# Two of four column groups of a gate product move from TensorE to VectorE, and the down projection's partial sums stay ungated until the last third

## The chip, the cores and the metric

The kernel runs on one core of a Trainium2 chip. The metric is the time in microseconds (us) of one execution on the device, as the median of several runs. The engines are named as in the profile: PE is TensorE's matrix multiplication, PEld its weight load, DVE VectorE, ACT ScalarE, POOL GpSimd, and SP SyncE, whose queue issues nearly all loads from HBM.

## What is computed

One inference step of a trunk layer on 128 context tokens and 128 latent tokens, D = 2048, feed-forward width 5632, all in fp32. Cut to what this change touches:

```python
mod = SiLU(cond) @ w_mod + b_mod     # 2 conditions (context, latent), 6 x 2048 columns
shift1, scale1, gate1, shift2, scale2, gate2 = split(mod, 6)
...                                  # mixer: scan branch, attention branch, x += gate1 * (...)
xm2 = RMSNorm(x) * (1 + scale2) + shift2
x = x + gate2 * ConvFFN(xm2)         # up projection (2 x 5632), centred conv of width 3,
                                     # a * SiLU(b), down projection (5632 -> 2048)
y = RMSNorm(x)
```

The change lies in gate2: how its 2048 columns are computed, and where in the feed-forward part they are multiplied in.

## The kernel before

**Weights.** Every weight comes as a stream of 512 KB tiles `raw` (128 partitions, two k-tiles of 512 columns) through a ring of five buffers (`RAW`). SP's queue issues the loads in the order of the program's list of steps; a load waits until the tile whose buffer it takes over has been read. `drive()` splits each weight tile into a rounded part `hi` (ACT, a copy, L184) and a remainder `lo` (DVE, a subtraction, L185), three buffers of each (`HL`), and PE multiplies three times: hi by low part, lo by high part, hi by high part, as an fp32 product.

**Feed-forward part.** It runs in three thirds (`CUT`: 8, 7 and 7 groups of 256 hidden columns and their 256 partners). In each third all *up groups* come first (`up_group`, 8 weight tiles each, called units here; PE lines L395 to L397, 24 matmuls of 256 columns per unit), then four *down groups* (`down_group`, one for each 512 output columns; L421 to L423). An up group accumulates in two PSUM banks, `h=0` and `h=1`, of a pool `acc` of three; so the second bank of the next group is one that the group before still has to give back. `evac()` empties them at every group's edge: for each of four pieces ACT writes a scaled copy into `ab` (L903) and DVE adds the two neighbours of the convolution (L904, L905), then come a SiLU (L906), the product (L907), and the split of the result (L909, L910). PE works through the first units of a group with `h=0` of three units ahead of `h=1` of the same three.

**Modulation product.** `mod_steps` computes mod in column groups of 512: the weights are PE's moving operand, the two condition vectors sit in a stationary operand of 32 columns, and each k-tile is put on one of four 32-column strips of PE (L263, `mod_mm`; unsplit fp32). A block of two raw tiles makes eight records in the profile. `mod_pp` then transposes the sums on DVE (L268), adds the four strips on PE (L272) and the bias on DVE (L276). Groups 20 to 23 are gate2; their 16 blocks are woven between the up units of the first third. At the end of these ups `load_g2` transposes the gate into rows, writes them to DRAM, and loads them back as four broadcast tiles `g2` (`gate_rows`, `gate_load`).

**Down groups.** After each down group of each third `down_evac` multiplies the sums in PSUM by the gate (L925) and adds the result to the residual `x1t` (L926): two DVE operations of 128x512 for each of the two sequences. In the last third ACT also takes the sum of squares there (L928), for the final norm, and DVE multiplies by that norm's weights (L929).

**Order.** Each engine executes its instructions in the order in which the built program has them. That order is set when the program is built, by a scheduler with priorities: `hi` and `lo` get a raised one (`HP`), everything else goes by the order of the steps.

Of the kernel before, what the change touches and what calls it, by code (L numbers as in the profile page):

```python
# [10 lines left out]
F32 = mybir.dt.float32  # L11
F32R = mybir.dt.float32r
I32 = mybir.dt.int32
AF = mybir.ActivationFunctionType
# [76 lines left out]
ATTP, ATTH, OLS = 1, 300, False  # L91
FF0, FF1, MF0, MF1 = 0.0, 1.0, 0.0, 1.0
G2A, G2B, G2S, G2C, LAG2, HP2 = 8, 8, 3, 2, 2, 1000
FIRST_BANKS = ("acc", "acc", "acc", "y")


@with_exitstack
def tile_hybrid_step(ctx, tc, a):
# [17 lines left out]
    def T4(shape, name, dt=F32):  # L116
        return w4.tile(shape, dt, tag="w4", name=name)
# [18 lines left out]
    def step(fn):  # L136
        steps.append(Step(fn))
# [180 lines left out]
    def mod_first(k0, n):  # L318
        v = a["w_mod_first"]
        st = {}  # L320
        nk = 8 // n
        view = lambda raw: raw.rearrange("p a c -> p (a c)").rearrange("p (k c) -> p k c", k=nk)

        def chunk(part, ku):
            def f(raw):
                if part == 0 and ku == 0:
                    st["a"] = PS([128, 2, 128 * n], "mod")
                r = view(raw)
                for j in range(nk):
# [7 lines left out]
        return [Step(chunk(p, ku), src(p, ku), False, "w4") for p in range(2) for ku in range(2 * n)]  # L337

    small = cpool.tile([128, 16], F32, name="small")
    nT = []  # L340
# [577 lines left out]
    G2 = []  # L918
    gfb = []

    def down_evac(acc, cg, s, last):
# [5 lines left out]
        if last:  # L927
            ACT(t, xv, AF.Square, accum_out=fs[:, 4 * s + cg:4 * s + cg + 1])  # L928
            TT(xv, xv, gfb[cg // 2][:, cs], OP.mult)  # L929

    def down_group(cg, ka, kb, last):
        st = {}

        def chunk(k0):
            def f(hi, lo):
                if k0 == ka:
                    st["a"] = [PS([128, 512], "acc", 3) for _ in range(2)]
                as_unit(st["a"], hi, lo, ff_lhs, k0, ka, kb)
                if k0 + 2 == kb:
                    for s in range(2):  # L940
                        down_evac(st["a"][s], cg, s, last)
                    if last and cg == 2:
                        norm_pre()
                        ACT(warm, fs[:, 6:7], AF.Sqrt)
            return f
        return [Step(chunk(k0), wsrc(a["w_down"], k0, 512 * cg)) for k0 in range(ka, kb, 2)]

    def down_last(cg, ka, kb):
        st = {"w": []}

        def chunk(k0):
            def f(hi, lo):
                if k0 == ka:
                    st["a"] = [PS([128, 512], "acc", 3) for _ in range(2)]
                st["w"].append((hi, lo))
                as_unit(st["a"], hi, lo, ff_lhs, k0, ka, kb, (0,))
                if k0 + 2 == kb:
                    for s in range(2):
                        if s:
                            for i, w in enumerate(st["w"]):  # L960
                                as_unit(st["a"], *w, ff_lhs, ka + 2 * i, ka, kb, (1,))
                        with tc.high_priority(HP2):
                            down_evac(st["a"][s], cg, s, True)
                            final(s)
            return f
        u = [Step(chunk(k0), wsrc(a["w_down"], k0, 512 * cg)) for k0 in range(ka, kb, 2)]
        for x in u[:len(u) - HL]:
            x.hl = XM
        return u
# [6 lines left out]
            gfb.append(t)  # L976

    CUT = [0, 8, 15, 22]
    g2s = mod_steps([20, 21, 22, 23])
    for x in g2s[:G2B]:  # L980
        x.pool = "first"

    def load_g2():
        gate_rows(80)
        for cg in range(4):
            G2.append(T4([128, 2, 512], "g2"))
            gate_load(80, cg, G2[cg])

    def behind(u):
        f = u.fn  # L990
# [11 lines left out]
    for p in range(3):  # L1002
# [3 lines left out]
        if p == 0:  # L1006
# [21 lines left out]
        if p == 2:  # L1028
            step(load_gf)
        for cg in range(4):  # L1030
            steps.extend((down_last if (p, cg) == (2, 3) else lambda *x: down_group(*x, p == 2))(cg, 2 * CUT[p], 2 * CUT[p + 1]))

    yout = [a["y_prompt"].rearrange("o t c -> (o t) c"), a["y_sample"].rearrange("o t c -> (o t) c")]

# [469 lines left out]
```

## Time and profile before

| | |
|---|---|
| median of 3 runs | 1549.94 us (1549.81 to 1554.12) |
| the profiled execution | 1552.15 us, its span 1550.1 us, mean PE clock 0.99 |
| PE, PEld busy | 1491.0 us (96%), 1311.1 us (85%) |
| DVE, ACT busy | 1007.7 us (65%), 766.7 us (49%) |
| POOL busy | 85.7 us (6%) |
| feed-forward part, first third | ups about 776 to 977 us, downs to 1066 |
| second third | ups about 1068 to 1229 us, downs to 1306 |
| last third | 1306 to the end |

A group of rows names a line, an engine and an operation, its output and inputs, how often it ran, and the mean duration. In an engine's timeline a row has its start, its duration and, in brackets, the idle time of that engine before it and what ended it. Where instructions of one engine follow each other without a gap, the distance of their starts is shorter than the duration that is printed; that distance is called the pitch here.

### The profile page before, as it was taken

Reading aid. Unit: us, or ns where it says so; the run is one execution under the profiler, and the core shown is the slowest. Engines: PE = TensorE matmul, PEld = TensorE weight load, DVE = VectorE, ACT = ScalarE, POOL = GpSimd, SP = SyncE. Lnnn points to the kernel's source line nnn. Section 1 sums busy time; section 2 is a strip of 40 time slices with the busy share of each in tenths; the row PEclk is TensorE's granted clock in tenths of the full one; section 3 lists DMA queues with packets and bytes.
Section 4 is the critical chain, followed back from the end, with each engine's and each line's share of the span. In section 5 each row is a group of like instructions: output and inputs, shape, how many; then the busy total and the mean of one; then the engine's idle time right before and its main releaser. Section 6 shows DMA issues by size and latency. Waiting matters only on the chain.

```text
span 1550.1 us, 29294 instructions
## 1 busy us (share of the span) xinstructions
PE 1491.0 (96%) x11871; PEld 1311.1 (85%) x11871; DVE 1007.7 (65%) x1541; ACT 766.7 (49%) x1191; POOL 85.7 (6%) x179
## 2 busy tenths in 40 slices
PE   6989999999899999999999999999999999999997
PEld 5758799778677788998689999889999988999986
DVE  4997776468866566765665656655665655666665
ACT  6335537645545666544554544433544543545543
POOL 2000004022321000000000000000000000000000
PEclk9999999999999999999999999999999999999999
DMA  9999754774676677975566676765555565566563
GB/s 352 352 340 321 286 196 157 258 277 156 209 241 238 240 250 274 310 244 192 172 242 235 205 245 201 238 200 190 176 192 181 181 197 191 175 205 197 170 203 123
DMA packets 104246, 349.18 MB, mean 225 GB/s; under 512 B 13900, under 2 KB 16628, under 8 KB 104112
## 3 DMA queue, kind: packets, MB, share of 16 engines
q1 hardware_dynamic: 98576, 344.20, 64.9%
q0 software_dynamic: 5312, 3.05, 0.8%
q8 instruction: 93, 1.52, 0.4%
q14 instruction: 41, 0.34, 0.1%
q10 hardware_dynamic: 224, 0.08, 0.0%
HBM read 343.76 MB, written 2.46 MB: 223 GB/s over the span
## 4 chain that ended last, share of the span: by engine, by line
PE 83%; DMA 8%; DVE 4%; ACT 2%; issue 1%; POOL 1%; SPq 0%; DVEq 0%; ACTq 0%
PE acc L395 16%; PE acc L396 16%; PE acc L397 16%; PE acc L421 8%; PE acc L422 8%; PE acc L423 8%; PE mod L263 5%; DMA raw<-in_w_mod_dram 2%; DMA raw<-in_w_in_dram 2%; PE bu L1375 1%; DVE lo L185 1%; DMA rw<-in_w_mod_dram 1%; DMA U<-u 1%; DMA raw<-in_w_attn_o_dram 1%; ACT hi L184 1%
## 5 line engine op out<-in xcount | busy, mean ns | idle before, releaser
L185 DVE TENSOR_TENSOR lo<-raw,hi 128x1024 fp32r<-128x1024 f32 (+1 forms) x456 | 538.7, 1186 | 444.8 <-ACT hi L184 442.8
L184 ACT ACTIVATE hi<-raw 128x1024 fp32r<-128x1024 f32 (+1 forms) x456 | 468.5, 1029 | 609.1 <-PE acc L397 260.7
L395 PE MATMUL acc<-yh,lo 128*128 128x256 f32 x1408 | 400.0, 284 | 0.0
L396 PE MATMUL acc<-yl,hi 128*128 128x256 f32 x1408 | 398.8, 283 | 0.0
L397 PE MATMUL acc<-yh,hi 128*128 128x256 f32 x1408 | 398.7, 283 | 0.0
L395 PEld LDWEIGHTS acc<-yh,lo 128*128 128x128 f32 x1408 | 270.3, 192 | 8.9 <-DVE lo L185 4.2
L396 PEld LDWEIGHTS acc<-yl,hi 128*128 128x128 f32 x1408 | 270.3, 192 | 0.1
L397 PEld LDWEIGHTS acc<-yh,hi 128*128 128x128 f32 x1408 | 270.2, 192 | 0.0
L395 PE MATMUL acc<-xh,lo 128*128 128x256 f32 x568 | 166.8, 294 | 9.3 <-ACT sig L672 4.8
L396 PE MATMUL acc<-xl,hi 128*128 128x256 f32 x568 | 163.4, 288 | 0.0
L397 PE MATMUL acc<-xh,hi 128*128 128x256 f32 x568 | 163.1, 287 | 0.0
L422 PE MATMUL acc<-lo,ff 128*128 128x512 f32 x352 | 136.8, 389 | 0.0
L423 PE MATMUL acc<-hi,ff 128*128 128x512 f32 x352 | 136.8, 389 | 0.0
L395 PEld LDWEIGHTS acc<-xh,lo 128*128 128x128 f32 x568 | 109.2, 192 | 31.4 <-DVE lo L185 6.9
L421 PE MATMUL acc<-hi,ff 128*128 128x512 f32 x352 | 127.8, 390 | 0.0
L396 PEld LDWEIGHTS acc<-xl,hi 128*128 128x128 f32 x568 | 109.6, 193 | 2.4 <-issue 2.2
L397 PEld LDWEIGHTS acc<-xh,hi 128*128 128x128 f32 x568 | 109.5, 193 | 0.7 <-issue 0.7
L263 PE MATMUL mod<-raw,cst 128*32 128x512 f32 x480 | 72.2, 631 | 8.0 <-DMA raw<-in_w_mod_dram 7.2
L421 PEld LDWEIGHTS acc<-hi,ff 128*128 128x128 f32 x352 | 66.1, 188 | 14.7 <-issue 1.1
L423 PEld LDWEIGHTS acc<-hi,ff 128*128 128x128 f32 x352 | 66.1, 188 | 13.7
L422 PEld LDWEIGHTS acc<-lo,ff 128*128 128x128 f32 x352 | 66.1, 188 | 13.5
L1316 POOL DMA_DIRECT2D U<-u x128 | 62.6, 497 | 159.6 <-PE bu L1375 138.5
(365 smaller groups left out, 2149.3 us busy)
## 6 DMA issues: line engine op xcount, KB each, us to landing
raw<-in_w_up_dram SPq DMA_DIRECT2D x176, 512.0 KB, 4.2
raw<-in_w_mod_dram SPq DMA_DIRECT2D x120, 512.0 KB, 5.1
raw<-in_w_in_dram SPq DMA_DIRECT2D x88, 512.0 KB, 4.5
raw<-in_w_down_dram SPq DMA_DIRECT2D x88, 512.0 KB, 4.3
rw<-in_w_mod_dram SPq DMA_DIRECT2D x56, 512.0 KB, 6.6
raw<-in_w_out_dram SPq DMA_DIRECT2D x32, 512.0 KB, 4.1
rw<-in_w_mod_first_dram SPq DMA_DIRECT2D x16, 512.0 KB, 7.4
raw<-in_w_in_dram SPq DMA_DIRECT2D x32, 256.0 KB, 6.1
```

Source lines behind the costliest of these rows:

```text
L184: ACT(th[:, w], raws[n][:, w], AF.Copy)
L185: TT(tl[:, w], raws[n][:, w], f32(th[:, w]), OP.subtract)
L263: return MM(acc[32 * j:32 * j + 32], cst[:, kt, 6 - 2 * b:38 - 2 * b], rhs, start=start, stop=stop, skip_group_check=True, tile_position=( ...
L395: MM(o, wl, xh, start=start, stop=False, skip_group_check=True)
L396: MM(o, wh, xl, start=False, stop=False, skip_group_check=True)
L397: MM(o, wh, xh, start=False, stop=stop, skip_group_check=True)
L421: MM(accs[s], xl, hi[:, j, :], start=(kt == first), stop=False)
L422: MM(accs[s], xh, lo[:, j, :], start=False, stop=False)
L423: lastmm[0] = MM(accs[s], xh, hi[:, j, :], start=False, stop=(kt == last - 1))
L1316: nc.gpsimd.dma_start(G["U4", qd][32 * e:32 * e + 32, q, :], u[32 * q:32 * q + 32, 64 * e:64 * e + 64])
L1375: MM(bu[:, ri, x], BL[d][:, ri, q, :], u[:, :, ::-1] if d else u, start=(x == 0), stop=True, skip_group_check=True)
```

## The change

Three things are changed.

- **Product.** Groups 22 and 23 of the modulation product (`G2P`) leave PE. `vec_mod` loads the same 16 raw tiles through the same ring, now woven into the first 0.8 of the *second* third's up units, and DVE computes them as running sums: for each of the two groups a tile `pacc` with two rows of 512 columns per partition (one per condition), to which each of the 16 k-tiles is added as weights times a per-partition scalar. That is 4 `tensor_scalar` and 60 `scalar_tensor_tensor` (STT) of 128x512. `done()` then sums over the partitions with four PE matmuls against a one-column selector (`onesel`), and a second `mod_pp` follows.
- **Gate rows.** Writing the gate's rows moves from the end of the first third's ups to the end of the second third's ups; the broadcast loads to the start of the last third.
- **Down sums.** The first third's down sums are copied ungated from PSUM into four tiles `ysum` by ACT, the second third's are added to them by DVE (one operation instead of two), and at the start of the last third `gate_sum` multiplies by the gate and adds to `x1t`: 16 DVE operations of 128x512. The last third is as before.

```diff
+G2P, POOLMOD = (22, 23), False
+    def vec_mod(gs):
+        n = 8 * len(gs)
+        st = {"raw": {}, "acc": []}
+        src = lambda i: wsrc(a["w_mod"], 2 * (i % 8), 512 * MOD_AT[gs[i // 8]])
...
+        def product(i, r):
+            if i % 8 == 0:
+                st["acc"].append(S4([128, 2, 512], "pacc"))
+            acc = st["acc"][-1]
+            for j in range(2):
+                kt = 2 * (i % 8) + j
+                for x in range(2):
+                    c = cst[:, kt, 6 + x:7 + x]
+                    if kt == 0:
+                        MODENG.tensor_scalar(acc[:, x], r[:, j], c, None, op0=OP.mult)
...
+                    else:
+                        STT(acc[:, x], r[:, j], c, acc[:, x], op0=OP.mult, op1=OP.add)
...
+            return Step(lambda raw: product(i, raw), src(i), False)
+        def done():
+            p = PS([128, 512], "mod")
+            m = 2 * len(gs)
+            with tc.issue_after(lastmm[0].ins):
+                for r in range(m):
+                    j = r % 4
+                    MM(p[32 * j:32 * j + 32], onesel[:, 7 - r:39 - r], st["acc"][r // 2][:, r % 2, :], start=r < 4, stop=r + 4 >= m,
+                       skip_group_check=True, tile_position=(0, 32 * j))
+            mod_pp(p, len(gs), [(4 * gs[0], 0, 4, 0, len(gs))])
+        return [unit(i) for i in range(n)], done
...
+    def down_part(acc, cg, s, p):
+        if len(ysum) < 4:
+            ysum.extend(T4([128, 1024], "ysum") for _ in range(4))
+        y = ysum[2 * s + cg // 2][:, 512 * (cg % 2):512 * (cg % 2) + 512]
+        if p:
+            TT(y, acc, y, OP.add)
+        else:
+            ACT(y, acc, AF.Copy)
+    def gate_sum(cg):
+        cs = slice(512 * (cg % 2), 512 * (cg % 2) + 512)
+        for s in range(2):
+            y, xv = ysum[2 * s + cg // 2][:, cs], x1t[2 * s + cg // 2][:, cs]
+            TT(y, y, G2[cg][:, s, :], OP.mult)
+            TT(xv, xv, y, OP.add)
...
-    g2s = mod_steps([20, 21, 22, 23])
+    g2s = mod_steps([g for g in range(20, 24) if g not in G2P])
+    g2u, g2done = vec_mod(list(G2P))
...
             weave(ups[8 - LAG2:], (g2s, 0.0, 0.8))
-            step(load_g2)
+        elif p == 1:
+            weave(ups, (g2u, 0.0, 0.8))
+            step(g2done)
+            step(lambda: gate_rows(80))
         else:
+            for cg in range(4):
+                step(lambda cg=cg: load_g2(cg))
             steps.extend(ups)
```

Three places of the built program show how the instructions stand. Lines have moved in the changed kernel: L371 is an accumulation of the product on DVE, L959 and L960 are the former L904 and L905, L962 and L965 the former L907 and L910, L186 the former L185, and L450 to L452 the former L395 to L397.

The first place is VectorE at an edge between two up groups of the second third. Before:

```order
L904 SCALAR_TENSOR_TENSOR ab_12450<-acc_12214,cw_118,ab_12450 128x2x127
L905 SCALAR_TENSOR_TENSOR ab_12450<-acc_12214,cw_118,ab_12450 128x2x127
L185 TENSOR_TENSOR lo_12469<-raw_12304,hi_12468 128x1024
L904 SCALAR_TENSOR_TENSOR ab_12450<-acc_12215,cw_118,ab_12450 128x2x127
L904 SCALAR_TENSOR_TENSOR ab_12450<-acc_12214,cw_118,ab_12450 128x2x127
L905 SCALAR_TENSOR_TENSOR ab_12450<-acc_12215,cw_118,ab_12450 128x2x127
L905 SCALAR_TENSOR_TENSOR ab_12450<-acc_12214,cw_118,ab_12450 128x2x127
L904 SCALAR_TENSOR_TENSOR ab_12450<-acc_12215,cw_118,ab_12450 128x2x127
L905 SCALAR_TENSOR_TENSOR ab_12450<-acc_12215,cw_118,ab_12450 128x2x127
L907 TENSOR_TENSOR ab_12450<-ab_12450 128x512
L185 TENSOR_TENSOR lo_12501<-raw_12334,hi_12500 128x1024
```

The third edge of the second third in the changed kernel:

```order
L959 SCALAR_TENSOR_TENSOR ab_12414<-acc_12153,cw_121,ab_12414 128x2x127
L960 SCALAR_TENSOR_TENSOR ab_12414<-acc_12153,cw_121,ab_12414 128x2x127
L186 TENSOR_TENSOR lo_12459<-raw_12345,hi_12458 128x1024
L959 SCALAR_TENSOR_TENSOR ab_12414<-acc_12154,cw_121,ab_12414 128x2x127
L371 SCALAR_TENSOR_TENSOR pacc_12377<-raw_12388,cst_105,pacc_12377 128x512 x2
L959 SCALAR_TENSOR_TENSOR ab_12414<-acc_12153,cw_121,ab_12414 128x2x127
L960 SCALAR_TENSOR_TENSOR ab_12414<-acc_12154,cw_121,ab_12414 128x2x127
L371 SCALAR_TENSOR_TENSOR pacc_12377<-raw_12388,cst_105,pacc_12377 128x512 x2
L960 SCALAR_TENSOR_TENSOR ab_12414<-acc_12153,cw_121,ab_12414 128x2x127
L959 SCALAR_TENSOR_TENSOR ab_12414<-acc_12154,cw_121,ab_12414 128x2x127
L960 SCALAR_TENSOR_TENSOR ab_12414<-acc_12154,cw_121,ab_12414 128x2x127
L962 TENSOR_TENSOR ab_12414<-ab_12414 128x512
```

Four accumulations now stand inside the evacuation of the banks.

The second place is SP's queue in the same stretch, where every row loads a weight tile. Before:

```order
L155 DMA raw_11874<-in_w_up_dram 128x1024
L155 DMA raw_11904<-in_w_up_dram 128x1024
L155 DMA raw_11952<-in_w_up_dram 128x1024
L155 DMA raw_11984<-in_w_up_dram 128x1024
L155 DMA raw_12014<-in_w_up_dram 128x1024
```

In the changed kernel:

```order
L156 DMA raw_12345<-in_w_up_dram 128x1024
L156 DMA raw_12375<-in_w_up_dram 128x1024
L156 DMA raw_12386<-in_w_up_dram 128x1024
L156 DMA raw_12388<-in_w_mod_dram 128x1024
L156 DMA raw_12462<-in_w_up_dram 128x1024
L156 DMA raw_12492<-in_w_up_dram 128x1024
L156 DMA raw_12502<-in_w_mod_dram 128x1024
L156 DMA raw_12504<-in_w_up_dram 128x1024
L156 DMA raw_12558<-in_w_up_dram 128x1024
```

The modulation tiles stand between the up weights. A load waits for the buffer that it takes over: that of raw_12502 for raw_12388's, which the last accumulation in the rows above frees. VectorE's next rows there are these:

```order
L371 SCALAR_TENSOR_TENSOR pacc_12377<-raw_12502,cst_105,pacc_12377 128x512 x2
L186 TENSOR_TENSOR lo_12489<-raw_12375,hi_12488 128x1024
L371 SCALAR_TENSOR_TENSOR pacc_12377<-raw_12502,cst_105,pacc_12377 128x512
L965 TENSOR_TENSOR ff_12429<-ab_12414,ff_12429 128x512
L371 SCALAR_TENSOR_TENSOR pacc_12377<-raw_12502,cst_105,pacc_12377 128x512
L186 TENSOR_TENSOR lo_12499<-raw_12386,hi_12498 128x1024
L186 TENSOR_TENSOR lo_12555<-raw_12462,hi_12554 128x1024
```

The first two read raw_12502, and the lo tile of the next unit stands behind them.

The third place is PE in the first third, at a block of the modulation product. Before:

```order
L396 MATMUL acc<-yl,hi 128x256
L397 MATMUL acc<-yh,hi 128x256
L263 MATMUL mod<-raw,cst 32x512 x4
L395 MATMUL acc<-yh,lo 128x256
L396 MATMUL acc<-yl,hi 128x256
L397 MATMUL acc<-yh,hi 128x256
```

The same place in the changed kernel:

```order
L452 MATMUL acc<-yh,hi 128x256
L450 MATMUL acc<-yh,lo 128x256
L451 MATMUL acc<-yl,hi 128x256
L452 MATMUL acc<-yh,hi 128x256
L450 MATMUL acc<-yh,lo 128x256
```

The block's four matmuls are gone; eight of the twelve blocks from here on leave PE in this way.

## Rows read from the trace of the kernel before

**Rows 1.** The page: busy time, share of the span and instructions of each engine.

```profile
PE 1491.0 (96%) x11871; PEld 1311.1 (85%) x11871; DVE 1007.7 (65%) x1541; ACT 766.7 (49%) x1191; POOL 85.7 (6%) x179
```

**Rows 2.** Windows: length, busy time by engine, PE clock, DMA share, GB/s.

```profile
776.00:977.00 201.00, 200.32 (x1647) 189.62 (x1644) 121.82 (x161) 97.11 (x122) 0.96 (x2) 0.99 0.66 226
977.00:1066.00 89.00, 89.00 (x400) 73.72 (x400) 52.23 (x57) 37.42 (x38) 0.00 (x0) 1.00 0.66 214
1068.00:1229.00 161.00, 161.00 (x1331) 160.47 (x1331) 97.26 (x120) 78.67 (x95) 0.00 (x0) 1.00 0.57 184
```

**Rows 3.** PE's timeline in the first third: start, duration, instruction, idle before.

```profile
801.11 0.28 PE L397 MATMUL acc<-yh,hi 128*128 128x256 f32 x1
801.32 1.07 PE L263 MATMUL mod<-raw,cst 128*32 128x512 f32 x8
...
802.54 0.28 PE L396 MATMUL acc<-yl,hi 128*128 128x256 f32 x1
...
809.00 1.07 PE L263 MATMUL mod<-raw,cst 128*32 128x512 f32 x8 [0.67 <-DMA raw<-in_w_mod_dram]
```

**Rows 4.** PE's timeline around a lone fp32 matmul of 512 columns (L658).

```profile
249.76 1.02 PE L658 MATMUL misc<-P,pg 128*128 128x512 f32 x2
...
250.74 0.28 PE L395 MATMUL acc<-xh,lo 128*128 128x256 f32 x1
```

**Rows 5.** PE's timeline around the four strip sums of `mod_pp`.

```profile
933.50 0.28 PE L397 MATMUL acc<-yh,hi 128*128 128x256 f32 x1
933.71 0.27 PE L272 MATMUL mod<-macc,kc 128*32 128x32 f32 x8
...
934.13 0.28 PE L396 MATMUL acc<-yl,hi 128*128 128x256 f32 x1
```

**Rows 6.** Groups by line and shape: count, busy us, mean ns, idle before.

```profile
L185 DVE TENSOR_TENSOR lo<-raw,hi 128x1024 fp32r<-128x1024 f32 x424 | 517.1, 1224 | 438.4 <-ACT hi L184 436.5
L904 DVE SCALAR_TENSOR_TENSOR ab<-acc,cw,ab 128x254 f32<-128x254 f32 x88 | 40.1, 477 | 6.2 <-ACT ab L903 6.0
L926 DVE TENSOR_TENSOR x1t<-x1t,dt 128x512 f32<-128x512 f32 x24 | 15.6, 685 | 0.1
L500 ACT ACTIVATE pg<-acc 128x512 f32<-128x512 f32 x12 | 7.0, 594 | 3.3 <-PE acc L423 2.1 <-PE acc L397 1.0
L844 DVE TENSOR_SCALAR n<-x1t,fs 128x512 f32<-128x512 f32 x6 | 2.8, 541 | 0.0
```

**Rows 7.** VectorE's timeline at the first group edge of the second third.

```profile
1088.90 1.23 DVE L185 TENSOR_TENSOR lo<-raw,hi 128x1024 fp32r<-128x1024 f32 x1 [0.74 <-ACT hi L184]
1090.04 0.87 DVE L904 SCALAR_TENSOR_TENSOR ab<-acc,cw,ab 128x254 f32<-128x254 f32 x2
1090.82 0.86 DVE L905 SCALAR_TENSOR_TENSOR ab<-acc,cw,ab 128x254 f32<-128x254 f32 x2
1091.93 0.48 DVE L904 SCALAR_TENSOR_TENSOR ab<-acc,cw,ab 128x254 f32<-128x254 f32 x1 [0.24 <-ACT ab L903]
...
1093.03 0.69 DVE L907 TENSOR_TENSOR ab<-ab 128x512 f32<-128x512 f32 x1
1094.66 1.23 DVE L185 TENSOR_TENSOR lo<-raw,hi 128x1024 fp32r<-128x1024 f32 x1 [0.94 <-ACT hi L184]
```

**Rows 8.** PE's timeline at the same edge.

```profile
1091.93 0.28 PE L395 MATMUL acc<-yh,lo 128*128 128x256 f32 x1
1092.05 0.28 PE L396 MATMUL acc<-yl,hi 128*128 128x256 f32 x1
```

**Rows 9.** Loads issued in the second third's ups: count, KB, median us to landing.

```profile
raw<-in_w_up_dram SPq DMA_DIRECT2D x49, 512.0 KB, 4.1
```

**Rows 10.** The same of the first third's ups, where modulation tiles are loaded too.

```profile
raw<-in_w_up_dram SPq DMA_DIRECT2D x60, 512.0 KB, 4.4
raw<-in_w_mod_dram SPq DMA_DIRECT2D x20, 512.0 KB, 4.4
```

**Rows 11.** Windows around idle time of PE, columns as in Rows 2.

```profile
512.00:516.00 4.00, 1.07 (x6) 0.16 (x5) 2.46 (x5) 3.91 (x9) 0.00 (x0) 1.00 0.98 365
516.00:520.00 4.00, 4.00 (x19) 2.83 (x20) 2.00 (x2) 2.92 (x4) 0.00 (x0) 0.57 0.08 28
604.00:608.00 4.00, 2.24 (x112) 2.01 (x114) 2.67 (x4) 3.97 (x5) 0.00 (x0) 1.00 0.61 195
```

**Rows 12.** VectorE's groups at 64 columns, both sources in SBUF.

```profile
L1103 DVE SCALAR_TENSOR_TENSOR wk<-wk 128x64 f32<-128x64 f32 x12 | 2.6, 219 | 0.0
L1171 DVE TENSOR_TENSOR M<-wk 128x64 f32<-128x64 f32 x5 | 1.1, 217 | 0.0
```

More of the change, by code (lines that the diff above doesn't have):

```diff
@@ L337, in mod_first, with load, unit, f @@
         return [Step(chunk(p, ku), src(p, ku), False, "w4") for p in range(2) for ku in range(2 * n)]
+    MODENG = nc.gpsimd if POOLMOD else nc.vector
+    onesel = cpool.tile([128, 40], F32, name="onesel")
+    nc.gpsimd.memset(onesel, 0.0)
+    nc.gpsimd.memset(onesel[:, 7:8], 1.0)
+    def vec_mod(gs):
+        n = 8 * len(gs)
+        st = {"raw": {}, "acc": []}
+        src = lambda i: wsrc(a["w_mod"], 2 * (i % 8), 512 * MOD_AT[gs[i // 8]])
+        def load(i):
+            if i < n:
+                st["raw"][i] = T4([128, 2, 512], "pw")
+                for o, x in src(i)(st["raw"][i]):
+                    nc.gpsimd.dma_start(o, x)
+        def product(i, r):
[8 more added lines that the diff above has]
+                        MODENG.tensor_scalar(acc[:, x], r[:, j], c, None, op0=OP.mult)
+                    elif POOLMOD:
+                        t = T2([128, 512], "pt")
+                        nc.gpsimd.tensor_scalar(t, r[:, j], c, None, op0=OP.mult)
+                        nc.gpsimd.tensor_tensor(acc[:, x], acc[:, x], t, OP.add)
+                    else:
+                        STT(acc[:, x], r[:, j], c, acc[:, x], op0=OP.mult, op1=OP.add)
+        def unit(i):
+            def f():
+                if i == 0:
+                    load(0)
+                load(i + 1)
+                product(i, st["raw"].pop(i))
+            if POOLMOD:
+                return Step(f)
+            return Step(lambda raw: product(i, raw), src(i), False)
[9 more added lines that the diff above has]
+        return [unit(i) for i in range(n)], done
     small = cpool.tile([128, 16], F32, name="small")
@@ L919, in tile_hybrid_step, with down_evac @@
     gfb = []
-    def down_evac(acc, cg, s, last):
+    ysum = []
+    def down_part(acc, cg, s, p):
[12 more added lines that the diff above has]
+            TT(xv, xv, y, OP.add)
+    def down_evac(acc, cg, s):
         cs = slice(512 * (cg % 2), 512 * (cg % 2) + 512)
@@ L926, in down_evac, with down_group @@
         TT(xv, xv, t, OP.add)
[L927 to L931, printed above, removed]
+        ACT(t, xv, AF.Square, accum_out=fs[:, 4 * s + cg:4 * s + cg + 1])
+        TT(xv, xv, gfb[cg // 2][:, cs], OP.mult)
+    def down_group(cg, ka, kb, p):
         st = {}
@@ L940, in f @@
                     for s in range(2):
-                        down_evac(st["a"][s], cg, s, last)
-                    if last and cg == 2:
+                        down_evac(st["a"][s], cg, s) if p == 2 else down_part(st["a"][s], cg, s, p)
+                    if p == 2 and cg == 2:
                         norm_pre()
@@ L962, in f @@
                         with tc.high_priority(HP2):
-                            down_evac(st["a"][s], cg, s, True)
+                            down_evac(st["a"][s], cg, s)
                             final(s)
@@ L978, in tile_hybrid_step, with load_g2 @@
     CUT = [0, 8, 15, 22]
-    g2s = mod_steps([20, 21, 22, 23])
+    g2s = mod_steps([g for g in range(20, 24) if g not in G2P])
+    g2u, g2done = vec_mod(list(G2P))
     for x in g2s[:G2B]:
         x.pool = "first"
[L983 to L987, printed above, removed]
+    def load_g2(cg):
+        G2.append(T4([128, 2, 512], "g2"))
+        gate_load(80, cg, G2[cg])
+        gate_sum(cg)
     def behind(u):
@@ L1024, in tile_hybrid_step @@
             weave(ups[8 - LAG2:], (g2s, 0.0, 0.8))
-            step(load_g2)
-        else:
+        elif p == 1:
+            weave(ups, (g2u, 0.0, 0.8))
+            step(g2done)
+            step(lambda: gate_rows(80))
+        else:
+            for cg in range(4):
+                step(lambda cg=cg: load_g2(cg))
             steps.extend(ups)
-        if p == 2:
             step(load_gf)
         for cg in range(4):
-            steps.extend((down_last if (p, cg) == (2, 3) else lambda *x: down_group(*x, p == 2))(cg, 2 * CUT[p], 2 * CUT[p + 1]))
+            steps.extend((down_last if (p, cg) == (2, 3) else lambda *x: down_group(*x, p))(cg, 2 * CUT[p], 2 * CUT[p + 1]))
     yout = [a["y_prompt"].rearrange("o t c -> (o t) c"), a["y_sample"].rearrange("o t c -> (o t) c")]
```

## The prediction

> **What bounds the kernel now.** The page comes first: PE is busy for 96% of the span, VectorE for 65% [rows 1]. That is an average over stages, so the windows of the feed-forward part come next: in the second third's ups PE is busy for 161.00 of 161 us, in the first third's for 200.32 of 201, at full clock [rows 2]. What is taken from PE there shortens the time, what PE waits for there lengthens it, one for one. VectorE has room on the mean: 97.26 of 161 us, for seven groups of 23.0 us, or 13.9 us busy and about 9 idle in each [rows 2]. The mean doesn't tell where in a group this room lies, so the third view is VectorE's timeline at a group's edge, held against PE's [rows 7, 8]. There the two meet closely. The third accumulator bank comes free with the second L905 of the pair, which ends at 1090.82 + 0.86 = 1091.68, and PE begins to write into it at about 1092.0. The slack is 0.25 to 0.35 us; I use 0.3.
>
> **What PE loses.** A block of eight records stands between L397 at 801.11 and L396 at 802.54 [rows 3]. Without it these two would be 0.24 us apart (a pitch of 0.12), so a block costs 1.43 - 0.24 = 1.19 us. Eight blocks go: 9.5 us. At one of them PE also waits 0.67 us for its weights [rows 3]; with some hundredths more at others I count 0.7. Sum: **-10.2 us**, all in a stretch where PE has no other gap.
>
> **What PE gains.** Four `onesel` matmuls of 512 columns. A lone one of that kind takes from 249.76 to 250.74 less one neighbour of 0.12, or 0.86 us [rows 4]. In the program two stand alone and two together on different strips, where a pair on four strips can't cost more than a block of eight: 2 x 0.86 + 1.1 = 2.9 us (bounds 2.4, if all strips overlap as in a block, and 3.4). The second strip sum costs 0.63 - 0.24 = 0.39 [rows 5]. Sum: **+3.3 us**. So PE's own work falls by about 6.9 us. That is what the change is worth if VectorE and the transfers hide all else.
>
> **What VectorE gains.** 64 operations of 128x512. For an STT of that width whose sources both lie in SBUF there is no row. L926, also two SBUF sources, takes 685 ns; durations exceed the pitch by 0.09 (L904: two in 0.87 with 477 each), which gives 0.60 us. From below, the one-source L844 gives 541 - 85 = 0.46; from above, a line through 64 columns at 219 and 254 columns at 477 gives 830 - 85 = 0.75 [rows 6, 7, 12]. I take 0.60, since STT and TT agree at 64 columns, 219 and 217 [rows 12]. 64 x 0.60 = 38 us come into 5.6 groups with about 9 us idle each, 50 us. VectorE stays below its limit, at some 90%. The amount is not the trouble, the place is.
>
> **Edges.** In the built program accumulations stand inside the evacuation. At the third and fourth edge it is four of them ahead of the L960 that frees the bank: 4 x 0.60 = 2.4, less 0.3 of slack, 2.1 us of PE's time at each. By the same count the first edge (three, and a lo tile that comes later) costs 1.65, the second 1.15, and the fifth, where a transpose and the bias addition of `mod_pp` stand inside, 0.8. Sum: **+7.8 us** (at 0.46 each 5.5, at 0.75 about 10).
>
> **Transfers.** At five of the edges' places a modulation tile takes over the buffer of the modulation tile before it, and between the accumulation that frees the buffer and the first one that needs the new tile stand only a few short operations. At the third edge these are L960, L959, L960 and L962: in the timeline before these reach from about 1091.2, where the second L905 of the pair begins, to the end of L907's pitch at 1093.03 + 0.60, or 2.4 us [rows 7]. The load takes 4.1 us in the second third, 4.4 where modulation tiles are loaded too [rows 9, 10]; I use 4.4. So VectorE stands for 2.0 us, then does two accumulations, 1.2, and only then the next lo tile, on which PE waits. Against this stand 0.94 us in which VectorE waits for hi there today [rows 7] and about 0.4 until PE needs the tile: 1.9 us on PE. The first, second and fourth edge and the place behind the fourth come to 1.1, 0.6, 1.6 and 0.8 in the same way. Sum: **+6.0 us** (5.4 with loads of 4.3, 7.4 with 4.6; 0 if the loads are issued early enough).
>
> The Trainium skill (DMA: Bandwidth & Descriptors, "Anatomy of one DMA") gives 2.0 us plus the bytes at 436 GB/s for a load issued by GpSimd, an estimate of 3.2 us for 512 KB; by it this sum would be about nothing, which is the first rival below. The medians of 4.1 and 4.4 us are longer [rows 9, 10].
>
> **Down groups: nothing.** In the first third's downs ACT's copy (about 0.59 each, L500) takes the place of two VectorE operations; ACT is busy for 37.42 of 89 us there and VectorE for 52.23 [rows 2, 6], and the copies come at a group's end, where the other bank gives PE a group's time. In the second third VectorE does one operation instead of two. The 16 operations of the last third (16 x 0.60 = 9.6 us) fall among the second third's last down groups and the last third's first units, spread over the four column groups; VectorE has over 40% free in down stages. If that cover failed, 9.6 us would be the bound; I add 1 us to the upper end. The gate's loads go past SP's queue some eight weight tiles ahead, and no wait stands behind them that isn't over by then.
>
> **Sum.** -10.2 + 3.3 + 7.8 + 6.0 = +6.9 us. The profiled execution took 1552.15 us, 2.2 more than the median of the runs; nothing in the sum depends on that, and I set it on the median: 1549.9 + 6.9, **1557 us**.
>
> **Rivals.**
> 1. *The transfers are hidden.* If the loads land in time, the edges alone are left: -10.2 + 3.3 + 7.8 = +0.9, 1551 us, no difference that can be seen. For it: half of the loads land sooner than the median of 4.1 [rows 9], and a PE that has just waited at an edge lets VectorE and ACT catch up. Against: the buffer is freed so late by the order, whatever the load takes. Chance 0.30, together with cheaper accumulations.
> 2. *The accumulations are hidden, faster.* VectorE has more idle time in the stretch (50 us) than it is given work (38). If the banks are given back in time in spite of the accumulations, PE keeps its 6.9 us: 1543 us. The place is the five edges; it decides at the point where their stalls sum to 2.2 us, below which the kernel is faster by over 0.3%. Against: four accumulations between L959 and L960 would have to fit into 0.3 us [rows 7, 8], and at the lower bound they take 1.8. Chance 0.08.
> 3. *The clock falls behind the stalls.* After a stretch in which PE was busy for 1.07 of 4 us the granted clock was 0.57 of full, nearer to 1.2 than to 2.4 GHz, for the next 4 us [rows 11]; after one with 2.24 busy of 4 it stayed at 1.00. At three edges two stalls of 2 us follow each other. A drop costs about 4 x 0.43 = 1.7 us; at three to five of them that makes 5 to 8 us more, 1562 to 1565 us. Chance 0.12.
> 4. *VectorE becomes the bound.* If an accumulation takes two times the 0.60, 64 x 1.2 = 77 us meet 50 us of idle time: +27, with -10.2 + 3.3 and some waits +21 to +25, about 1573 us. Rows 12 speak against it: at 64 columns both forms take the same. The Trainium skill (Vector Engine (DVE) Microarchitecture Reference, "Points that are easy to get wrong") says just this of an STT with two non-bf16 sources in SBUF, that its throughput is halved; the 219 ns beside 217 don't bear it out. Chance 0.03.
>
> **Chances and range.** Forecast 0.47 (1553 to 1561), the rivals 0.30, 0.08, 0.12 and 0.03. A measurement of this kernel tells 0.3%, 4.65 us, from no change. Faster: 0.08. The same (1545.3 to 1554.6): the first rival and the low end of the forecast, 0.34. Slower: 0.58. The range reaches from 1547, the first rival with accumulations of 0.46 us and less slack lost, to 1566, the third one's end: outside lie the second, the fourth and some of the third, 0.15 to 0.2.
>
> **What would show it.** Right: PE's timeline has gaps of about 2 us at the five group edges of the second third's ups and none in the first third's, the first ones ended by L960, the later ones by lo, with VectorE waiting there for a modulation load; VectorE near 90% in that stretch; the first third's ups shorter by about 10 us; an accumulation of about 0.69 us. Wrong: edges without gaps (rival 2), VectorE never waiting for a load (rival 1), a clock under 0.9 in the stretch (rival 3), an accumulation near 1.3 us (rival 4), or gaps of PE in the down groups, where I expect none.

## The result, and the profile after

The changed kernel is slower. The median of nine runs is 1565.23 us, beside 1549.94 for nine runs of the kernel before; the ratio is 1.0089 with a 95% interval of 1.0067 to 1.0112, or 10 to 17 us. The profiled execution took 1571.71 us (span 1569.9), 19.6 more than the profiled one before.

The page of the changed kernel, busy time by engine, to be held against [rows 1]:

```profile
PE 1495.8 (95%) x11823; PEld 1318.6 (84%) x11823; DVE 1042.8 (66%) x1599; ACT 771.1 (49%) x1199; POOL 85.8 (5%) x181
```

Busy time says nothing here: PE has 48 instructions fewer and is busy for longer. A matmul at the lower clock counts with a longer time (0.41 us at 1093 us, against 0.28 elsewhere). The stages say more. The table has the time from the first matmul of one stage to the first of the next, taken from PE's timelines of the two profiled executions.

| stage | before | after | difference |
|---|---|---|---|
| up to the first up matmul | 776.3 | 779.7 | +3.4 |
| first third, ups | 201.0 | 192.8 | -8.2 |
| first third, downs | 87.3 | 88.4 | +1.1 |
| second third, ups | 161.3 | 184.8 | +23.5 |
| second third, downs | 76.4 | 76.4 | 0.0 |
| last third, ups | 161.3 | 161.3 | 0.0 |
| last downs and end | 86.6 | 86.6 | 0.0 |

By this table the second third's ups before run from 1064.6 to 1225.9 us; the windows from 1068 and to 1229 of [rows 2] and of the table of stages lie some 3 us late, with PE busy throughout in both. The 3.4 us ahead of the feed-forward part lie in code that the change leaves alone, and in the nine profiled executions of this document that part starts anywhere between 773.4 and 782.3 us. So the change took 8.2 us in the first third's ups and lost 24.6 from there to the end of the second third's ups. Windows of the changed kernel over its first third's ups and its second third's ups (columns as in [rows 2]):

```profile
780.00:972.00 192.00, 191.31 (x1576) 188.81 (x1576) 120.45 (x160) 95.96 (x121) 0.00 (x0) 0.98 0.58 192
1061.00:1245.00 184.00, 170.05 (x1356) 164.64 (x1357) 133.77 (x177) 78.08 (x95) 0.96 (x2) 0.98 0.60 206
```

In the second row PE stands for 14 of 184 us, where it stood for none in [rows 2]. PE's timeline names the places: these are all its rows from 790 us to the end of the second third's ups with a wait of over 0.6 us ahead of them.

```profile
1060.85 0.39 PE L450 MATMUL acc<-yh,lo 128*128 128x256 f32 x1 [0.89 <-DVE lo L186]
...
1090.71 0.58 PE L450 MATMUL acc<-yh,lo 128*128 128x256 f32 x1 [2.54 <-DVE lo L186]
...
1118.41 1.04 PE L389 MATMUL mod<-pacc,onesel 128*32 128x512 f32 x2 [1.47 <-DVE pacc L371]
...
1127.48 0.39 PE L450 MATMUL acc<-yh,lo 128*128 128x256 f32 x1 [0.76 <-DVE lo L186]
...
1148.85 0.36 PE L450 MATMUL acc<-yh,lo 128*128 128x256 f32 x1 [2.39 <-DVE ab L960]
...
1154.44 0.39 PE L450 MATMUL acc<-yh,lo 128*128 128x256 f32 x1 [1.04 <-DVE lo L186]
...
1176.46 0.36 PE L450 MATMUL acc<-yh,lo 128*128 128x256 f32 x1 [2.85 <-DVE ab L960]
...
1197.09 0.39 PE L450 MATMUL acc<-yh,lo 128*128 128x256 f32 x1 [1.64 <-DVE lo L186]
```

The first stands at the start of the stage, the last at the start of the sixth group, and the others at the first four group edges and up to two units behind them. Two are ended by L960, which gives a bank back, the others by a lo tile or by the last accumulation of the first running sum. VectorE's timeline at the third edge shows both kinds in one piece; it answers to [rows 7]:

```profile
1144.42 0.47 DVE L959 SCALAR_TENSOR_TENSOR ab<-acc,cw,ab 128x254 f32<-128x254 f32 x1
1144.81 1.40 DVE L371 SCALAR_TENSOR_TENSOR pacc<-raw,cst,pacc 128x512 f32<-128x512 f32 x2
1146.13 0.47 DVE L959 SCALAR_TENSOR_TENSOR ab<-acc,cw,ab 128x254 f32<-128x254 f32 x1
1146.52 0.47 DVE L960 SCALAR_TENSOR_TENSOR ab<-acc,cw,ab 128x254 f32<-128x254 f32 x1
1146.91 1.40 DVE L371 SCALAR_TENSOR_TENSOR pacc<-raw,cst,pacc 128x512 f32<-128x512 f32 x2
1148.23 0.47 DVE L960 SCALAR_TENSOR_TENSOR ab<-acc,cw,ab 128x254 f32<-128x254 f32 x1
...
1149.72 0.69 DVE L962 TENSOR_TENSOR ab<-ab 128x512 f32<-128x512 f32 x1
1151.84 1.41 DVE L371 SCALAR_TENSOR_TENSOR pacc<-raw,cst,pacc 128x512 f32<-128x512 f32 x2 [1.43 <-DMA raw<-in_w_mod_dram]
1153.17 1.22 DVE L186 TENSOR_TENSOR lo<-raw,hi 128x1024 fp32r<-128x1024 f32 x1
```

Four accumulations stand ahead of the L960 that ends at 1148.70, and PE goes on at 1148.85. The last pair ends at about 1148.2 and frees its tile's buffer; VectorE goes on with the next tile 3.6 us later, after standing for 1.43 us. The lo tile behind it ends at 1154.39, and PE goes on at 1154.44.

The accumulations, and what VectorE waited for ahead of them:

```profile
L371 DVE SCALAR_TENSOR_TENSOR pacc<-raw,cst,pacc x60: 740/745/753, 1051.2 to 1197.6; 128x512 f32<-128x512 f32 x60
...
  DMA raw<-in_w_mod_dram: 25.0, 12
```

The 25.0 us are a sum over twelve waits; 21.6 of them lie behind 1060 us, the rest in the last down group ahead of it, where the first accumulations stand. And the granted clock around the first and the third edge (window, busy times, then PE's clock as the third number from the right):

```profile
1088.00:1092.00 4.00, 1.46 (x8) 1.29 (x7) 4.00 (x7) 0.25 (x1) 0.00 (x0) 0.76 0.38 117
1092.00:1096.00 4.00, 3.97 (x19) 3.71 (x19) 3.02 (x7) 1.50 (x3) 0.00 (x0) 0.50 0.63 246
1096.00:1100.00 4.00, 4.00 (x32) 4.00 (x32) 3.92 (x6) 2.95 (x4) 0.00 (x0) 0.89 0.00 0
1144.00:1148.00 4.00, 2.46 (x21) 2.26 (x19) 4.00 (x8) 0.71 (x2) 0.00 (x0) 1.00 0.56 182
1148.00:1152.00 4.00, 3.15 (x26) 3.18 (x27) 2.43 (x6) 2.07 (x3) 0.00 (x0) 1.00 0.37 135
```

Behind the first edge's wait PE ran at 1.2 GHz in the whole second window and in parts of its neighbours, which cost about 0.4 + 2.0 + 0.4 = 2.8 us (busy time by the share of clock that is missing). Behind the third edge's it stayed at 2.4 GHz.

### The profile page after: what moved, and what is told of

It reads as the page before. It is cut to its first block, busy times and chain, and to the rows that moved or that the text cites. A ratio compares the mean times of both kernels' runs of the same rounds, so it can differ in the third digit from the quotient of the medians.

```text
span 1569.9 us, 29274 instructions
## 1 busy us (share of the span) xinstructions
PE 1495.8 (95%) x11823; PEld 1318.6 (84%) x11823; DVE 1042.8 (66%) x1599; ACT 771.1 (49%) x1199; POOL 85.8 (5%) x181
## 4 chain that ended last, share of the span: by engine, by line
PE 76%; DMA 11%; DVE 7%; ACT 3%; issue 2%; POOL 0%; SPq 0%; DVEq 0%; ACTq 0%
PE acc L450 14%; PE acc L451 14%; PE acc L452 14%; PE acc L476 8%; PE acc L477 8%; PE acc L478 8%; DMA raw<-in_w_mod_dram 6%; PE mod L264 4%; DVE lo L186 3%; DMA raw<-in_w_in_dram 2%; DVE pacc L371 2%; PE bu L1451 1%; DMA U<-u 1%; ACT hi L185 1%; PE misc L1384 1%
## 5 line engine op out<-in xcount | busy, mean ns | idle before, releaser
L186 DVE TENSOR_TENSOR lo<-raw,hi 128x1024 fp32r<-128x1024 f32 (+1 forms) x456 | 537.6, 1185 | 404.9 <-ACT hi L185 401.4
L185 ACT ACTIVATE hi<-raw 128x1024 fp32r<-128x1024 f32 (+1 forms) x456 | 468.5, 1029 | 603.0 <-PE acc L452 267.7
L450 PE MATMUL acc<-yh,lo 128*128 128x256 f32 x1408 | 402.4, 286 | 13.1 <-DVE lo L186 7.5
L451 PE MATMUL acc<-yl,hi 128*128 128x256 f32 x1408 | 400.8, 285 | 0.0
L452 PE MATMUL acc<-yh,hi 128*128 128x256 f32 x1408 | 400.7, 285 | 0.0
L450 PEld LDWEIGHTS acc<-yh,lo 128*128 128x128 f32 x1408 | 272.1, 193 | 20.0 <-DVE lo L186 11.0
L451 PEld LDWEIGHTS acc<-yl,hi 128*128 128x128 f32 x1408 | 272.3, 193 | 0.0
L452 PEld LDWEIGHTS acc<-yh,hi 128*128 128x128 f32 x1408 | 272.3, 193 | 0.0
L450 PE MATMUL acc<-xh,lo 128*128 128x256 f32 x568 | 167.6, 295 | 7.7 <-ACT sig L727 4.1
L451 PE MATMUL acc<-xl,hi 128*128 128x256 f32 x568 | 164.2, 289 | 0.0
L452 PE MATMUL acc<-xh,hi 128*128 128x256 f32 x568 | 163.7, 289 | 0.0
L450 PEld LDWEIGHTS acc<-xh,lo 128*128 128x128 f32 x568 | 110.0, 194 | 30.6 <-issue 7.3
L451 PEld LDWEIGHTS acc<-xl,hi 128*128 128x128 f32 x568 | 110.4, 194 | 2.4 <-issue 2.2
L452 PEld LDWEIGHTS acc<-xh,hi 128*128 128x128 f32 x568 | 110.1, 194 | 0.7 <-issue 0.7
L478 PEld LDWEIGHTS acc<-hi,ff 128*128 128x128 f32 x352 | 66.1, 188 | 13.8
L958 ACT ACTIVATE ab<-acc,cw 128x256 f32<-128x256 f32 x88 | 47.2, 559 | 59.1 <-DVE ab L960 48.8
L264 PE MATMUL mod<-raw,cst 128*32 128x512 f32 x416 | 62.8, 625 | 11.0 <-DMA raw<-in_w_mod_dram 10.8
```

The costliest lines, as they stand in the source:

```text
L185: ACT(th[:, w], raws[n][:, w], AF.Copy)
L186: TT(tl[:, w], raws[n][:, w], f32(th[:, w]), OP.subtract)
L264: return MM(acc[32 * j:32 * j + 32], cst[:, kt, 6 - 2 * b:38 - 2 * b], rhs, start=start, stop=stop, skip_group_check=True, tile_position=( ...
L450: MM(o, wl, xh, start=start, stop=False, skip_group_check=True)
L451: MM(o, wh, xl, start=False, stop=False, skip_group_check=True)
L452: MM(o, wh, xh, start=False, stop=stop, skip_group_check=True)
```

## The experiments

Three theories were held against each other: **A**, the one of the prediction (the accumulations' place at the edges, and loads that take over a buffer too late); **B**, that VectorE simply has too much to do; **C**, that the ungated sums cost. One run has a fourth, **D**: that the late loads alone make the loss. Times of one chip are compared by their ratio to the kernel before on the same chip, whose median lay at 1554.5 and 1554.8 us in the two sets of runs below.

**The down sums alone.** All four groups of the product go back to PE:

```diff
-G2P, POOLMOD = (22, 23), False
+G2P, POOLMOD = (), False
```

> The down sums of two thirds stay ungated as in the changed kernel, but all four groups of the gate's product run on TensorE in the first third, as before. Theory A (the loss comes from the accumulations' place on VectorE and from their late loads): nothing of that is here, so 1550 us, a ratio to the kernel before of 0.997 to 1.003, the second third's ups back at 161 us. Rival C (the ungated sums, their copies on ScalarE and the 16 late gate operations cost): 5 us or more above it, ratio over 1.003, with gaps of TensorE in the down groups or at the start of the last third.

Measured: ratio 0.9997 (0.9974 to 1.0020). All stages last as before, the second third's ups 161.27 us, with PE busy in all of the window that held 14 us of idle time above:

```profile
1061.00:1245.00 184.00, 184.00 (x1445) 179.81 (x1444) 110.80 (x135) 89.66 (x108) 0.00 (x0) 1.00 0.60 188
```

C falls: the ungated sums cost nothing and bring nothing. The loss belongs to the product.

**Own buffers for the modulation tiles.** VectorE keeps all 64 operations:

```diff
-        cap = {"raw": RAW, "w4": LOADS, "first": 8, "s4": G2S}
+        cap = {"raw": RAW, "w4": LOADS, "first": 8, "s4": G2S, "pm": 3}
...
-                r = (T4 if c.pool == "first" else S4)([128, 2, 512], "rw4")
+                r = (T4 if c.pool in ("first", "pm") else S4)([128, 2, 512], "rw4")
...
-            return Step(lambda raw: product(i, raw), src(i), False)
+            return Step(lambda raw: product(i, raw), src(i), False, "pm")
```

> The changed kernel, with its 16 modulation tiles in three buffers of their own instead of the weights' ring, so that each load is issued long before its use; VectorE has the same 64 operations, and the built order now holds none of them inside the first and the fourth edge's evacuation, one inside the second and four inside the third. Theory A: VectorE no longer waits for a modulation load and the edges cost 0, 1, 2.5 to 3, 0 us: -10.2 + 3.9 for TensorE's matmuls + 4 = -2 us, 1546 to 1551 us, no clock drop. Rival B (VectorE has simply too much to do in the second third, 0.66 us x 64 = 42 us in groups with 9 us idle each): the loss stays, 1558 to 1566 us.

Measured: ratio 0.9975 (0.9960 to 0.9990), 4 us faster than before instead of 14 slower. The two largest sums of VectorE's waits in the second third's ups (total us, times, longest):

```profile
DVE lo L186 <- ACT hi L185: 34.5, 27, 2.1
DVE macc L269 <- PE mod L389: 1.2, 1, 1.2
```

No wait for a modulation load is left, and VectorE has 34.5 us in which it only waits for ACT's hi tiles. B falls with that: the same amount of work fits. The amount of loads falls too, since the 16 tiles still come through in this stage. PE stands once in the stage, at the third edge, where three accumulations and a lo tile lie between the first L959 and the L960 that frees the bank, and a fourth accumulation just ahead:

```profile
1134.95 0.35 PE L450 MATMUL acc<-yh,lo 128*128 128x256 f32 x1 [1.80 <-DVE ab L960]
```

The stage lasts 167.6 us (+6.3) and the first third's ups 191.0 (-10.0); the sum of -3.7 us is the measured gain. The expectation of -2 came near by terms that made up for each other. The selector matmuls stood in two pairs and cost 2.3 us with 0.4 for the strip sum, not 3.9; the edges cost 2.0 instead of 4; but the clock, which was expected to stay, fell behind the one wait, which cost some 1.5 us:

```profile
1136.00:1140.00 4.00, 4.00 (x26) 4.00 (x25) 1.89 (x3) 1.99 (x3) 0.00 (x0) 0.65 0.25 101
```

The edit changes two things at once, the loads and the order at the edges; the run with short sums takes them apart from the other side.

**Evacuation first.** Own buffers, and besides:

```diff
-                    evac()
+                    with tc.high_priority(HP):
+                        evac()
```

> As the one with own buffers, and the evacuation of an up group's banks gets the same raised priority as the hi and lo tiles. In the built order only the third edge still holds accumulations, three of them ahead of the operation that frees the bank and one behind it. Theory A: the third edge costs about 2 us, the others nothing: -10.2 + 3.9 + 2 = -4 us, 1544 to 1548 us. Rival B: 1558 to 1566 us as before.

Measured: ratio 0.9982 (0.9960 to 1.0004). The third edge has two waits of 0.80 and 0.75 us in place of one of 1.80; no gain over own buffers alone can be told. One reason shows in PE's timeline: the four selector matmuls stand alone here, at 1.17 us each, where the run with own buffers has two pairs at 1.17, so that 2.3 us go there. B falls here too, and nothing speaks against A; the raised priority alone brought nothing that can be seen.

**Short sums.** Loads and buffers as in the changed kernel; the kernel leaves out most columns of the product, so that VectorE's work is cut (w is 64, or 512 for the first tile of a group):

```diff
+            w = 512 if i % 8 == 0 else 64
...
-                        STT(acc[:, x], r[:, j], c, acc[:, x], op0=OP.mult, op1=OP.add)
+                        STT(acc[:, x, 0:w], r[:, j, 0:w], c, acc[:, x, 0:w], op0=OP.mult, op1=OP.add)
```

> The changed kernel, with 56 of the 64 operations of the running sums over 64 columns instead of 512 (the other columns of these products are left out); loads, buffers and all else as they are. Theory A: an accumulation takes 0.15 us instead of 0.66, so the edges shrink to some tenths, but the buffers still pass from one modulation tile to the next and part of the load waits stays: of 14.8 us of waits 3 to 8 are left, 1547 to 1553 us. Rival D (the loads alone make the loss, VectorE's own time nothing): 1558 us or more. Rival B: all waits go, 1543 to 1545 us.

Measured: ratio 1.0012 (0.9988 to 1.0035), within A's range and outside those of B and D. A short accumulation took 280 ns at a pitch of 0.20, not 0.15. VectorE's two largest sums of waits in the second third's ups:

```profile
DVE pacc L372 <- DMA raw<-in_w_mod_dram: 31.1, 13, 4.8
DVE lo L186 <- ACT hi L185: 29.1, 23, 1.8
```

VectorE waits longer for modulation tiles (31.1 us) than in the changed kernel (21.6), and PE still stands for 7.6 us behind it, at eight places that are all ended by a lo tile and none by an L960 (here L961). The longest is 1.47 us, and the clock stays at 1.00 in the whole stage. So late loads with nearly no work on VectorE make some 8 us of waits, and the rest of the changed kernel's 13 to 15 (13.3 us as the trace names them) needs VectorE's time.

**The changed kernel again**, without an edit, for the clock:

> The changed kernel once more, unaltered, for a second profile of it. Theory A: the same waits in the second third's ups, 14 to 16 us in the same places, since the order is fixed; the drop of the clock at the first edge, which cost 3.4 us in the first profile, need not come back, so these ups last 20 to 24 us longer than before. If the drop comes back in the same place, it belongs to the change like the waits (it follows the first edge's gap); if it is absent, it is an accident of that execution.

Measured: ratio 1.0102 (1.0073 to 1.0131). The waits sum to the same (13.3 us as the trace names them, both times), and most places are the same, but not the sizes. Two grew:

```profile
1089.10 0.58 PE L450 MATMUL acc<-yh,lo 128*128 128x256 f32 x1 [3.46 <-DVE lo L186]
...
1175.56 0.55 PE L450 MATMUL acc<-yh,lo 128*128 128x256 f32 x1 [4.42 <-DVE ab L960]
```

These were 2.54 and 2.85 us in the first profile. In return the 1.04 us behind the third edge are gone and others are shorter. The drop of the clock came back at the first edge, and others joined it:

```profile
1085.00:1089.00 4.00, 0.64 (x6) 0.43 (x4) 3.56 (x6) 0.00 (x0) 0.00 (x0) 0.89 0.39 158
1089.00:1093.00 4.00, 3.87 (x16) 3.61 (x17) 3.79 (x10) 1.76 (x3) 0.00 (x0) 0.50 0.70 252
...
1142.00:1146.00 4.00, 1.99 (x17) 1.78 (x15) 4.00 (x9) 0.56 (x1) 0.00 (x0) 1.00 0.47 163
1146.00:1150.00 4.00, 3.62 (x18) 3.65 (x19) 2.42 (x5) 1.31 (x2) 0.00 (x0) 0.57 0.41 131
```

The third edge's wait of 2.39 us, the same as in the first profile, was followed by a clock of 0.57 this time. The first profile in windows that lie alike to that wait:

```profile
1144.47:1148.47 4.00, 1.99 (x17) 1.79 (x15) 4.00 (x9) 0.56 (x1) 0.00 (x0) 1.00 0.48 152
1148.47:1152.47 4.00, 3.62 (x30) 3.65 (x31) 2.43 (x5) 2.54 (x4) 0.00 (x0) 1.00 0.36 131
```

With those behind the fourth edge the drops cost 6.8 us, summed over their windows as above (the 3.4 us of the expectation are the drop that was put at 2.8 there). The second third's ups lasted 187.4 us, 26.1 longer than before and more than the 20 to 24 that were expected. So the clock's falls belong to the change, but which wait brings one differs from execution to execution.

**The product in the down groups**, through the ring as in the changed kernel:

```diff
-            weave(ups, (g2u, 0.0, 0.8))
...
+        if p < 2:
+            weave(downs, (g2u[8 * p:8 * p + 8], 0.0, 0.8))
```

> The same product through the same ring of five buffers, but its 16 tiles are woven into the down groups of the first two thirds, eight each, and the gate's loads and the gated sums into the ups of the last third. Theory A (place): a down group has no edge as close as an up group's, so the accumulations hide better; but buffers still pass from one modulation tile to the next, so some load waits remain: first third's ups 10 us shorter, downs 2 to 8 us longer in sum, and up to 3 us at the last third's edges, where the gated sums stand: 1546 to 1556 us. Rival B (VectorE's amount alone decides): downs have 40 us free for 21 us of work each, so nothing is lost there: 1543 to 1546 us.

Measured: ratio 1.0059 (1.0035 to 1.0082), above both expectations. The first third's ups gained 10.9 us and the other ups kept their time within 0.6 us, but the downs lost 6.3 and 12.7 us, the latter with the selector matmuls. Two of the largest waits of PE, and windows over the two down stages:

```profile
980.41 0.47 PE L476 MATMUL acc<-hi,ff 128*128 128x512 f32 x1 [2.87 <-DVE ab L960]
...
1276.78 0.50 PE L477 MATMUL acc<-lo,ff 128*128 128x512 f32 x1 [2.12 <-DVE lo L186]
...
972.00:1066.00 94.00, 89.99 (x390) 73.48 (x389) 63.57 (x75) 40.55 (x44) 0.00 (x0) 0.98 0.65 224
1227.00:1316.00 89.00, 81.52 (x347) 64.89 (x346) 62.78 (x78) 33.12 (x34) 0.00 (x0) 0.96 0.64 213
```

The first is an edge that the expectation had forgotten: the last up group is evacuated beside the first down units, and there accumulations stood inside again, six of them; the second third's last group has the same (2.86 us). The second is a lo tile behind a modulation load that VectorE waited for. With VectorE busy for 63.57 of 94 and 62.78 of 89 us, some 30% free, B, by which nothing is lost in the downs, falls once more. The clock fell as well behind both waits of 2.9 us.

**Behind units 1, 3 and 5, selector matmuls together**, own buffers:

```diff
-            weave(ups, (g2u, 0.0, 0.8))
+            fill = list(g2u)
+            for k, u in enumerate(ups):
+                steps.append(u)
+                if k % 8 in (0, 2, 4) and fill:
+                    steps.append(fill.pop(0))
...
+            for r in (3, 0, 1, 2):
+                with tc.issue_after(prev.ins):
```

> As the one with own buffers, but the product's tiles stand behind the first, third and fifth unit of each up group, so that the built order holds no accumulation between the first L959 and the bank's release at the first, fourth and fifth edge and at most two at the others; and three of the four selector matmuls stand together. Theory A: -10.2 for the blocks, +2.4 for the selector matmuls, +0.4 for the second strip sum, +0.5 to 1.5 for the edges: -6 to -7 us, 1542 to 1545 us, a ratio of 0.995 to 0.9965. Rival B: no better than with own buffers alone, 0.9975.

Measured: ratio 0.9977 (0.9962 to 0.9993), as with own buffers alone, which is B's number, and short of A's. The selector matmuls stand in two places, but so they did in the run with own buffers, so nothing was won there. And three edges now have a wait of 0.7 to 0.9 us each (L451, L960 and L961 are L450, L959 and L960 of the changed kernel):

```profile
1112.04 0.38 PE L451 MATMUL acc<-yh,lo 128*128 128x256 f32 x1 [0.69 <-DVE lo L186]
...
1137.89 0.36 PE L451 MATMUL acc<-yh,lo 128*128 128x256 f32 x1 [0.93 <-DVE ab L961]
...
1162.08 0.36 PE L451 MATMUL acc<-yh,lo 128*128 128x256 f32 x1 [0.93 <-DVE ab L961]
```

Two, one and no accumulation stand inside there. VectorE at the last of the three:

```profile
1156.90 0.49 DVE L960 SCALAR_TENSOR_TENSOR ab<-acc,cw,ab 128x254 f32<-128x254 f32 x1
1157.97 1.23 DVE L186 TENSOR_TENSOR lo<-raw,hi 128x1024 fp32r<-128x1024 f32 x1 [0.59 <-ACT hi L185]
...
1159.50 0.86 DVE L961 SCALAR_TENSOR_TENSOR ab<-acc,cw,ab 128x254 f32<-128x254 f32 x2
...
1161.46 0.87 DVE L961 SCALAR_TENSOR_TENSOR ab<-acc,cw,ab 128x254 f32<-128x254 f32 x2
```

Here the built order has put the first L961 behind a lo tile that VectorE had to wait for; before the change it stands ahead of that tile. B is not the reason, since VectorE waited for ACT's hi tiles for 34.3 us in this stage. What counts is when VectorE gets to the operation that frees the bank, and the whole order around it decides on that; the count of accumulations inside was too simple a measure.

## Why the prediction came out as it did

The forecast was +7 us (1557), the measurement is +14 by the ratio (1565 by the medians): the direction and the places were right, the size was half. The measured time lies outside the forecast's own 1553 to 1561 and at the figure of rival 3; the wide range holds it only because its upper end, 1566, was drawn for that rival.

- **What PE loses, -10.2 us.** Right. The seven profiles without the eight blocks show the first third's ups shorter by 8.2 to 10.9 us. They differ by how long the clock stays low at the stage's start, one window of 4 us or two (it cost the profiled execution before 1.4 us, the changed kernel's 3.1, both by busy time and missing share); with that taken out, the gain is 9.9 to 10.8 us, 9.9 in the changed kernel.
- **What PE gains, +3.3 us.** Undersized, 3.9 (and by a slip: 2 x 0.86 + 1.1 is 2.8, not 2.9). PE's timeline of the changed kernel around the second selector matmul, which answers to [rows 4]:

```profile
1120.96 0.28 PE L452 MATMUL acc<-yh,hi 128*128 128x256 f32 x1
1121.17 1.05 PE L389 MATMUL mod<-pacc,onesel 128*32 128x512 f32 x2
...
1122.37 0.28 PE L451 MATMUL acc<-yl,hi 128*128 128x256 f32 x1
```

It costs 1.41 - 0.24 = 1.17 us, and the pair at 1198.72 costs the same 1.17 as each of the two lone ones: 3.5 in sum, and 0.4 for the second strip sum. The 0.86 of [rows 4] was for a matmul of another shape, with 128 stationary columns.
- **What VectorE gains.** An accumulation takes 745 ns with a pitch of 0.66, not 0.60; it lies inside the bounds of 0.46 and 0.75. With 745 ns for 512 columns, and 280 ns for 64 in the run with short sums, a further column costs 1.04 ns, as much as in a TENSOR_TENSOR (685 and 217 ns, [rows 6, 12]). What an accumulation takes beyond L926 and L1103, whose times the prediction went by, is 60 ns at either width (745 against 685, 280 against 219); no run shows why. Rival 4 falls. The Trainium skill (Vector Engine (DVE) Microarchitecture Reference, "Points that are easy to get wrong") states a halved throughput for an STT with two non-bf16 sources in SBUF. These rows don't show it.
- **Edges, +7.8 us, and transfers, +6.0 us.** Right in place and nearly in sum: 13.8 forecast, 14.8 of waits in the ups and 1.0 at their start measured (gaps beyond the pitch in PE's timeline of the first profile). By place, an edge with what follows it: 2.7 us at the first edge (2.75 forecast), 2.6 at the second (1.75), 3.8 at the third (4.0), 3.0 at the fourth (3.7), 1.8 behind it (0.8), nothing at the fifth (0.8), and 0.9 inside the first group, where nothing was forecast. By what ended them the split was off, and the near match of the sums is in part luck: L960 ended 5.6 us where the edges were put at 7.8, lo tiles 7.6 where the loads were put at 6.0, and 1.6 lie at the first selector matmul, which waits for the last accumulation and was in no term. At the first two edges no bank was waited for. At the third VectorE stood for 1.43 us, not 2.0, since the tile came 3.6 us after its buffer was free and not 4.4. (The "about nothing" that the prediction gives for its estimate of 3.2 us is, by its own working at the third edge, 0.8 + 1.2 - 0.94 - 0.4 = 0.7.) And VectorE was busy for 103.38 of the 137 us from 1061 to 1198, 75% and not near 90.
- **Down groups, nothing.** Right, but for the 1.0 us in front of the second third's ups. The down sums alone changed no stage.
- **The clock, counted at nothing in the sum.** This is the step that was mis-sized most. The prediction saw rows in which the clock fell behind idle time [rows 11], and made of it a rival of its own, with a chance of 0.12, instead of a term that comes on top of the forecast. Waits of over 2 us at the edges brought drops in both profiles of the changed kernel, worth about 3 and 7 us. With them (3 to 7), the selector matmuls (0.6) and the longer waits (2.0) the sum of +6.9 becomes +12.5 to +16.5. Both profiles are of long executions, the first of the longest of its nine, so that the clock's price in the median one is not known. That it isn't theirs alone shows in the mean granted clock of all runs: 0.986 for the nine of the changed kernel, 0.989 and 0.990 for the 31 and 17 of the kernel before in the two sets.

Rival 1 (the transfers hidden) was tried by giving the tiles their own buffers: with the loads early the kernel is faster than before by 0.25%, some 4 us, where that rival gave +0.9; but the order at the edges was another there too. Rival 2's 1543 us was reached by no run. What wasn't tried is a kernel with the changed kernel's own order at the edges and early loads; so the split of the 14.8 us into 8 from the loads and the rest from the accumulations rests on the run with short sums, where the order was not quite the same; it is argued, not shown.

## What to carry to other kernels

Work that goes to an engine with idle time on the mean is worth what is saved only if it keeps out of the moments at which the bound engine waits for that one: look at the tightest edge, count what the built order puts in front of the operation that frees a buffer there, and hold it against the slack. A tile that another engine consumes in its own order should not share a short ring with the stream that feeds the bound engine; here the same 64 operations cost 14 us through the ring and gave 4 with three buffers of their own and the order that came with them. And where a change makes waits of about 2 us on TensorE, the clock's fall belongs in the sum, as a term and not as another case: of the twelve waits of 1.5 us or more in the feed-forward parts of these profiles seven were followed by one.

## What was not expected of the hardware

A wait of the same length (2.39 us, at the same instruction, with the engine busy for 1.99 of 4 us around it in both cases) left the clock at 1.00 in one execution and was followed by 0.57 in another. With own buffers a single wait of 1.80 us was followed by a window at 0.65, while 2.85 us left it at 1.00 in the first profile of the changed kernel. A matmul with a 32-column stationary operand between matmuls of 128 columns cost 1.17 us whether one or two of them stood together on different strips, and 1.18 where three did.
